# Queries and keys of seven head pairs as 2x2 block products ahead of the attention, in a two-branch encoder block

## The chip, the cores and the metric

One Trainium2 chip, one NeuronCore of it. The time is device microseconds of one execution; lower is better. PE is TensorE's matmul, PEld its weight load, DVE is VectorE, ACT ScalarE, POOL GpSimd, SP SyncE, which here issues most DMAs.

## The reference

One encoder layer on 1024 positions of 1024 channels, float32. Only the part up to the attention is touched by the change:

```python
h = rmsnorm(x, g_mix[i]) * (1 + scale1) + shift1
proj = h @ w_in[i]
qa, ka, va, qb, kb, vb, ga, gb = jnp.split(proj, split_at, axis=-1)
oa = mixture_of_dilations(heads(qa), heads(ka), heads(va), rel_bias)        # 8 heads of 64
ob = neighbourhood_attention_2d(heads(qb), heads(kb), heads(vb), na_rpb[i]) # 8 heads of 64
merged = jax.nn.sigmoid(ga) * (oa @ w_branch_dil) + jax.nn.sigmoid(gb) * (ob @ w_branch_na)
x = x + gate1 * (merged @ w_out[i])
...                                                                         # then a convolutional FFN
```

`w_in` has 40 column tiles of 128: 4 each of queries, keys and values of the dilated branch, 4 each of the neighbourhood branch, and 16 of gates. A tile of queries or keys holds one pair of heads.

## The kernel before

**Precision.** A float32 product is made of three matmuls of reduced-precision parts: `hi` is an operand rounded by ACT, `lo` what is left, by a subtraction on DVE or POOL; hi·hi, hi·lo and lo·hi are summed in PSUM (`product`, lines 84 to 86).

**Stages.** First (0 to 142 us) the modulated `h` is made, in two halves of 512 positions (`scaled`, `modulate`), then the values of all heads and the queries and keys of head pair 0. Then comes the attention, then the merge of the branches, `w_out`, and the FFN. The FFN's up and down projections already use block products in seven steps (`a_operands`, `products`, lines 1363 to 1365).

**Attention in slots.** It runs in 100 numbered slots. 64 belong to the dilated branch, eight per head; from slot 64 on the neighbourhood branch has four per head. In a slot PE makes scores `S` (from `qs`, `ks`, `kl`); DVE adds the bias and takes the minimum (L690, L1017); ACT takes exponentials (L691, L1019); two slots later PE turns the weights (`T`), ACT and DVE split them (`th` L698, `tl` L699), and in the slot after that PE multiplies by the values (`O`). A finished head output is taken by ACT and then DVE (`u`, L733 and L734; L1057 and L1061). In the neighbourhood branch DVE and POOL also normalise the weights (L1023, L1026).

**Filling.** Between these PE does other work in steps of three matmuls (`fill_steps`): 30 column tiles, 14 of queries and keys for the coming pairs and 16 of gates, each 16 steps (two halves, eight blocks of K). The loop at the end gives a slot 4, 8, 6 or 4 steps, spread over four places. For the neighbourhood queries `q_step` writes two half-wide matmuls in place of one, to reorder positions. Queries and keys are evicted by `q_evict` and `k_evict`, a half head at a time, into tiles for scores; keys are copied to the other partitions by DMA.

**Order.** PE, ACT and DVE run in the order in which the attention's code is written; SP and POOL are ordered by a scheduler. Work that isn't due at one moment (evictions, weight splits `whi`, value splits `vv`, outputs `u`, gate evictions `gs`) waits in a queue of pairs: `aside(ns, one, two)`. After each fill step `catch_up(550)` first emits all `two` parts of what was emitted before (DVE's half), then as many `one` parts (ACT's half) as 550 ns pay for. So the places of the fill steps set the places of these instructions.

**A pair's weights.** Per dilated pair, DVE writes row sums that go through DRAM and come back twice (`turn`, `factors`, `shares`, `weigh`), three and four slots later.

Of the kernel before, what the change touches and what calls it, by code (L numbers as in the profile page):

```python
# [29 lines left out]
def hybrid_encoder(tc, xT, c, w_ada, small, w_in, p1_bias, p23_bias, na_bias, ln2_mult, ident, w_br, w_out,  # L30
# [202 lines left out]
    def modulate(x, hf, ks, pb):  # L233

        last = ()
        for k in [*ks, None]:
# [7 lines left out]
            last = k is not None and (lo, t, b, f(hi))  # L244

    def scaled(x, k):

        hi, lo = h[0, k] = h_tile(), h_tile()
        t, b, g = stage[k % 2], ada[:, k:k + 1], am1[:, k:k + 1]
        act.activation(hi, x, AF.Identity, bias=b, scale=g)  # L250
# [106 lines left out]
    def at_once(ns, one, two=lambda: None):
        one()
        two()

    def q_evict(br, qk, hf, p, later=at_once):
        parts = []
        for i in range(2):
            a, b = slice(64 * i, 64 * i + 64), slice(64 - 64 * i, 128 - 64 * i)
            d, pp = qk[0][i][:, halves[hf]], p
            if br:
                d = qk[0][i].rearrange("p (v r t) -> p v r t", v=64, r=4)[:, :, 2 * hf:2 * hf + 2]
                pp = p.rearrange("p (r v t) -> p v r t", r=2, v=64)
            parts.append((d[a], d[b], pp[a]))

        def one():
            for da, db, pp in parts:
                act.activation(da, pp, AF.Copy)

        def two():
            for da, db, pp in parts:
                dve.tensor_tensor(db, pp, f(da), OP.subtract)
        later(1200, one, two)

    def k_evict(br, qk, hf, p, later=at_once):  # L380
        parts = []
        for i in range(2):
            a = slice(64 * i, 64 * i + 64)
            kh, ll, pp = qk[1][i][:, halves[hf]], qk[2][i][:, halves[hf]], p
            if br:
                kh, ll = (t.rearrange("p (w t r) -> p r w t", w=16, t=16)[:, 2 * hf:2 * hf + 2]
                          for t in (qk[1][i], qk[2][i]))
                pp = p.rearrange("p (r w t) -> p r w t", r=2, w=16)
            parts.append((kh[a], ll[a], pp[a]))

        def one(heads=(0, 1)):
            for kh, ll, pp in [parts[i] for i in heads]:
                act.activation(kh, pp, AF.Copy, scale=0.125)

        def two(heads=(0, 1)):
            for kh, ll, pp in [parts[i] for i in heads]:
                dve.scalar_tensor_tensor(ll, pp, 0.125, f(kh), OP.mult, OP.subtract)
            for i in heads:
                a, b = slice(64 * i, 64 * i + 64), slice(64 - 64 * i, 128 - 64 * i)
                for t in (qk[1][i], qk[2][i]):  # L400
                    if br == 0:
                        sp.dma_start(f(t)[b, halves[hf]], f(t)[a, halves[hf]])
                    elif hf:
                        sp.dma_start(f(t)[b], f(t)[a])
        if br == 0:
# [13 lines left out]

    def q_step(br, p, w, hf, k):  # L420
        if br == 0:
            product(p, w, lambda k: h[hf, k], ks=[k])
            return
        mhi, mlo = (t.rearrange("p (r w c t) -> p r c w t", r=2, w=16, c=4) for t in h[hf, k])
        for x, (ww, m) in enumerate(((w[0], mhi), (w[0], mlo), (w[1], mhi))):
            for r in range(2):
                pe.matmul(p[:, 256 * r:256 * r + 256], ww[:, k], m[:, r], start=k + x + r == 0,  # L427
                          stop=k == KT - 1 and x == 2, skip_group_check=True)
# [8 lines left out]
    def vb_chunks(cb):  # L437
        t0, n = NA_T0[cb], NA_NC[cb]
        for r in range(4):
            sp.dma_start(vb_s[cb].rearrange("(w t r) n -> r w t n", r=4, t=n)[r],  # L440
                         vb_c[256 * r:256 * r + 256].rearrange("(w t) n -> w t n", t=16)[:, t0:t0 + n])

    with tc.manual_schedule(engines={e.engine for e in (sp, act, dve, pool, pe)}):
# [53 lines left out]
        for q in range(4):  # L497
# [6 lines left out]
            low = [scaled(x[0][k], k) for k in ks]  # L504
            if q == 0:
# [104 lines left out]

        done_rows = 0
        folds = folds_in(early.tile([128, 512], FT, name="mt", bufs=3), 4)
        due = []
        for n, step in enumerate(v_steps[:10]):
            if step is None:
# [19 lines left out]
            done_rows = row_ends[n]  # L635
        act.activation(wpool.tile([128, KT], FT, name="rs", bufs=2), cs, AF.Exp)
# [4 lines left out]
        sm_pool = tc.alloc_tile_pool(name="sm", bufs=2, reuse_waits="tile")  # L641
        lnm = sm_pool.tile([128, 384], FT, name="lnm", bufs=1)
        sp.dma_start(lnm, ln2_mult)
        loads = [dil_loads(head) for head in range(2)]
# [15 lines left out]
    first_w = w_split(ahead.pop(1), pool)  # L660
# [4 lines left out]
    ps_n.release()  # L665

# [91 lines left out]
    class DilHead:  # L758
        def __init__(self, pair, pr, i, s0, u, st):
# [208 lines left out]
    class NaHead:  # L968
# [97 lines left out]
    def fill_steps():  # L1066
        jobs = []
        for n, gates in enumerate((2, 2, 2, 2, 2, 1, 1, 4)):
            if n < 7:
                br, pr = divmod(n + 1, 4)  # L1070
                jobs += [(x_ + pr, "qk"[y], n + 1) for y, x_ in enumerate(((0, 4), (12, 16))[br])]
            g0 = sum(1 for j in jobs if j[1] == "g")
            jobs += [(24 + g0 + t, "g", g0 + t) for t in range(gates)]
        w, raw = first_w, {1: ahead.pop(jobs[1][0])}
        w_mark = 0
        marks = [0, 0]
        for n, (t, kind, to) in enumerate(jobs):
            ensure(w_mark)
            if n + 1 < len(jobs):
                w_next = [wpool.tile([128, KT, 128], FR, name=x_) for x_ in ("whi", "wlo")]  # L1080
                w_mark = side_split(raw.pop(n + 1), *w_next)
            if n + 2 < len(jobs):
                raw[n + 2] = w_load(w_in[jobs[n + 2][0]])
            if kind == "q":
# [890 lines left out]
```

## Time and profile before

| | |
|---|---|
| runs (3), median | 1477.52 us (1476.70 to 1478.46) |
| span of the profiled execution | 1474.0 us (the page has no other time of it) |
| mean granted TensorE clock | 0.998 |
| moved by DMA | 210.75 MB, mean 143 GB/s |
| the chain that ended last | PE 90%, DVE 3%, DMA 3%, ACT 2% |
| S of the dilated branch | from 142.0 us |
| S of the neighbourhood branch | from 416.9 us |

The span runs from the first to the last instruction; the run times hold what lies around it too. Matmuls in a row overlap in the trace (a 512-wide one has 0.39 us and the next starts 0.23 us later), so the price of one is the distance of two starts. An idle time in brackets stands before the instruction, with the one that released it.

### The profile page before, as it was taken

How to read it: one execution, taken by the hardware profiler on the slowest of the kernel's cores; microseconds unless marked ns; L12 is line 12 of the kernel's file. 1: busy time of each engine (PE TensorE's matmuls, PEld its weight loads, DVE VectorE, ACT ScalarE, POOL GpSimd, SP SyncE). 2: the span in 40 equal slices, each digit the busy share in tenths (PEclk: the TensorE clock that was granted, in tenths of full speed). 3: DMA queues.
4: the chain of work that ended last, by engine and by line, in shares of the span. 5: the costliest groups of instructions: out<-in, count | busy, mean ns of one | idle time of the engine just before them, and what ended most of it. 6: DMA issues, size and time to landing. Idle time of an engine off the chain costs nothing.

```text
span 1474.0 us, 21562 instructions
## 1 busy us (share of the span) xinstructions
PE 1459.1 (99%) x7584; PEld 1242.1 (84%) x7584; DVE 943.2 (64%) x1775; ACT 775.8 (53%) x1448; POOL 766.6 (52%) x640
## 2 busy tenths in 40 slices
PE   9999999999999999999999999999999999999998
PEld 8888888889898998888888778888888888888888
DVE  7785546555654656466516897666666667787865
ACT  5522666666655666553346554444444447575543
POOL 4132333333234454422268678766676676989712
PEclk9999999999999999999999999999999999999999
DMA  9587325354736556587553313222222234542313
GB/s 371 199 305 260 91 84 129 99 136 126 194 110 176 142 147 172 164 260 256 192 165 127 107 53 133 86 86 86 86 73 81 72 130 142 200 128 87 107 41 115
DMA packets 121173, 210.75 MB, mean 143 GB/s; under 512 B 46660, under 2 KB 59588, under 8 KB 121028
## 3 DMA queue, kind: packets, MB, share of 16 engines
q1 hardware_dynamic: 119064, 206.41, 44.1%
q10 hardware_dynamic: 2000, 2.95, 0.5%
q8 instruction: 60, 0.98, 0.3%
q14 instruction: 49, 0.40, 0.1%
HBM read 163.58 MB, written 43.12 MB: 140 GB/s over the span
## 4 chain that ended last, share of the span: by engine, by line
PE 90%; DVE 3%; DMA 3%; ACT 2%; issue 1%; POOL 0%; SPq 0%; DVEq 0%; ACTq 0%; POOLq 0%
PE pj L1363 12%; PE pj L1364 12%; PE pj L1365 12%; PE pj L84 11%; PE pj L86 11%; PE pj L85 11%; PE pj L427 2%; PE O L1048 2%; PE T L1035 1%; PE S L1013 1%; PE pv L301 1%; PE pv L300 1%; PE pv L302 1%; PE O L876 1%; PE O L825 1%; PE T L859 1%
## 5 line engine op out<-in xcount | busy, mean ns | idle before, releaser
L61 POOL TENSOR_TENSOR wlo<-wraw,whi 128x512 fp32r<-128x512 f32 (+1 forms) x84 | 106.3, 1288 | 145.2 <-ACT whi L57 143.4
L84 PE MATMUL pj<-h,whi 128*128 128x512 f32 x432 | 178.0, 412 | 0.1
L86 PE MATMUL pj<-h,wlo 128*128 128x512 f32 x432 | 169.7, 393 | 0.0
L85 PE MATMUL pj<-h,whi 128*128 128x512 f32 x432 | 169.4, 392 | 0.0
L1364 PE MATMUL pj<-op,wsh 128*128 128x512 f32 x408 | 158.7, 389 | 0.5 <-DVE op L1290 0.5
L1363 PE MATMUL pj<-op,wsh 128*128 128x512 f32 x408 | 158.4, 389 | 0.5 <-ACT wsh L57 0.5
L1365 PE MATMUL pj<-op,wsl 128*128 128x512 f32 x408 | 157.4, 389 | 0.0
L699 DVE TENSOR_TENSOR tl<-T,th 128x512 fp32r<-128x512 f32 (+3 forms) x120 | 77.3, 654 | 106.9 <-ACT th L698 105.7
L749 POOL TENSOR_TENSOR wlo<-wraw,whi 128x512 fp32r<-128x512 f32 x58 | 74.2, 1294 | 131.7 <-ACT whi L748 131.7
L61 POOL TENSOR_TENSOR wsl<-big,wsh 128x512 fp32r<-128x512 f32 (+1 forms) x86 | 112.0, 1325 | 45.6 <-ACT wsh L57 40.7
L691 ACT ACTIVATE P<-P,st 128x256 f32<-128x256 f32 x128 | 64.2, 502 | 87.2 <-DVE st L690 87.2
L1599 DVE SCALAR_TENSOR_TENSOR big<-pj,sm,big 128x512 f32<-128x512 f32 (+2 forms) x183 | 94.9, 562 | 16.6 <-ACT big L1593 15.6
L86 PEld LDWEIGHTS pj<-h,wlo 128*128 128x128 f32 x432 | 81.1, 188 | 18.0
L84 PEld LDWEIGHTS pj<-h,whi 128*128 128x128 f32 x432 | 81.5, 189 | 11.3 <-issue 0.5
L1363 PE MATMUL pj<-op,whi 128*128 128x512 f32 x232 | 90.7, 391 | 0.2 <-ACT wc L1369 0.2
L1363 PEld LDWEIGHTS pj<-op,wsh 128*128 128x128 f32 x408 | 76.6, 188 | 16.9 <-ACT wsh L57 1.0
L1364 PEld LDWEIGHTS pj<-op,wsh 128*128 128x128 f32 x408 | 76.6, 188 | 16.7 <-DVE op L1290 0.9
L1365 PE MATMUL pj<-op,wlo 128*128 128x512 f32 x232 | 90.3, 389 | 0.0
L1364 PE MATMUL pj<-op,whi 128*128 128x512 f32 x232 | 90.3, 389 | 0.0
L85 PEld LDWEIGHTS pj<-h,whi 128*128 128x128 f32 x432 | 81.6, 189 | 10.1
L1365 PEld LDWEIGHTS pj<-op,wsl 128*128 128x128 f32 x408 | 76.6, 188 | 16.1 <-POOL wsl L61 0.2
L61 POOL TENSOR_TENSOR wsl<-wraw,wsh 128x384 fp32r<-128x384 f32 (+1 forms) x46 | 57.1, 1262 | 57.5 <-ACT wsh L57 49.9
(423 smaller groups left out, 4160.1 us busy)
## 6 DMA issues: line engine op xcount, KB each, us to landing
wraw<-w_in SPq DMA_DIRECT2D x32, 512.0 KB
wada<-w_ada SPq DMA_DIRECT2D x31, 512.0 KB
big<-w_up SPq DMA_DIRECT2D x22, 512.0 KB
wraw<-w_up SPq DMA_DIRECT2D x22, 512.0 KB
big<-as SPq DMA_DIRECT2D x22, 512.0 KB
as<-big SPq DMA_DIRECT2D x21, 512.0 KB
gs<-gs SPq DMA_DIRECT2D x32, 256.0 KB
g<-gs SPq DMA_DIRECT2D x16, 512.0 KB
```

What stands on the lines that cost most here:

```text
L61: lo_eng.tensor_tensor(lo[:, i:i + step], raw[:, i:i + step], f(hi)[:, i:i + step], OP.subtract)
L84: pe.matmul(psum, whi[:, k0 + k], mhi, start=k == 0, stop=False)
L85: pe.matmul(psum, whi[:, k0 + k], mlo, start=False, stop=False)
L86: pe.matmul(psum, wlo[:, k0 + k], mhi, start=False, stop=k == n - 1)
L427: pe.matmul(p[:, 256 * r:256 * r + 256], ww[:, k], m[:, r], start=k + x + r == 0, stop=k == KT - 1 and x == 2, skip_group_check=True)
L691: act.activation(pp, pp, AF.Exp, bias=mi, scale=-1.0, accum_out=li)
L699: dve.tensor_tensor(tl[:m, :n], pt[:m, :n], f(th)[:m, :n], OP.subtract)
L749: pool.tensor_tensor(lo[:, i:i + n], raw[:, i:i + n], f(hi)[:, i:i + n], OP.subtract)
L1363: pe.matmul(psum, whi[:, k], bhi, start=j < 4 and k == 0, stop=False, skip_group_check=True)
L1364: pe.matmul(psum, whi[:, k], blo, start=False, stop=False, skip_group_check=True)
L1365: pe.matmul(psum, wlo[:, k], bhi, start=False, stop=k == n - 1, skip_group_check=True)
L1599: dve.scalar_tensor_tensor(y[:, dst], src, wt, y[:, dst], OP.mult, OP.add)
```

## The change

Queries and keys of pairs 1 to 7 leave the filling. They are made in a stage of their own between the values and the attention, in the order 4, 5, 6, 7, 1, 2, 3. For a pair, the query tile and the key tile are the two block rows of the stationary operand, the halves of K its two block columns; the halves of positions are the block columns of `h`. Seven block products of 12 matmuls each replace eight (`STEPS`, moved up in the file). This needs:

- raw (unsplit) `h`, kept by extra ACT instructions (`keep_scaled`, and a line in `modulate`), four sums of blocks on POOL (`t_sums`, eight instructions of 1024 columns), and their splits (`t_split`: 16 times ACT, then DVE or POOL);
- per pair, three POOL sums, one DVE sum and seven halves of splits on ACT and POOL (`a_operands`), and five DVE additions and an ACT copy on PSUM (`products`);
- evictions of whole tiles, both heads at once (`qk_evict`, `na_evict`), stored in DRAM (`q_scr`), hi and lo, and loads by pair (`qk_load`), eight slots ahead of a pair's first slot.

In the attention 16 gate tiles are left: 256 steps. Five come ahead of slot 0, then 2, 4, 3 or 2 per slot, in fewer places: with two steps, one stands after the turns and one at the slot's end. `qk_marks` and the evictions in the slots are gone.

```diff
@@ modulate, scaled
+            if k is not None:
+                act.activation(raw_h[hf][k // 2][:, k % 2], t, AF.Identity, bias=b)
...
+    def keep_scaled(x, k):
+        act.activation(x, x, AF.Identity, bias=ada[:, k:k + 1], scale=am1[:, k:k + 1])
...
@@ evictions
+    def split_qk(y, dst, src):
+        hi, lo = dst
+        act.activation(hi, src, AF.Copy, scale=(1.0, 0.125)[y])
+        if y:
+            dve.scalar_tensor_tensor(lo, src, 0.125, f(hi), OP.mult, OP.subtract)
+        else:
+            dve.tensor_tensor(lo, src, f(hi), OP.subtract)
+
+    def qk_evict(pr, y, hf, p, tag):
+        st = qkpool.tile([128, 2, 512], FR, name=tag)
+        split_qk(y, (st[:, 0], st[:, 1]), p)
+        sp.dma_start(q_scr[pr, 2 * y:2 * y + 2].rearrange("x p s -> p x s")[:, :, halves[hf]], f(st))
...
+    def qk_load(pr):
+        qk = qk_tiles()
         for i in range(2):
             a = slice(64 * i, 64 * i + 64)
...
+            sp.dma_start(f(qk[0][i]), q_scr[pr, 0:2, a])
+            for y in range(2):
+                for b in range(2):
+                    sp.dma_start(f(qk[1 + y][i])[64 * b:64 * b + 64], q_scr[pr, 2 + y, a])
+        return qk
...
@@ sums of the blocks of h
+        def t_sums():
+            (a0, a1, c0, c1), (b0, b1, d0, d1) = raw_h
+            for a, b in ((a0, b0), (a1, b1)):
+                pool.tensor_tensor(a, b, a, OP.subtract)
+            for b, d in ((b0, d0), (b1, d1)):
+                pool.tensor_tensor(b, d, b, OP.subtract)
+            for a, d in ((a0, d0), (a1, d1)):
+                pool.tensor_tensor(d, d, a, OP.subtract)
+            for c, d in ((c0, d0), (c1, d1)):
+                pool.tensor_tensor(c, c, d, OP.subtract)
...
@@ the new stage, ahead of the attention
+    gens = [p_products(n, (0, 4, 1, 2, 3, 5, 6)) for n in range(2)]
+    for _ in range(2):
+        for g in gens:
+            advance(g)
+    t_split("T4", rpool, h0[2:], (dve, pool))
+    for n in range(len(order)):
+        if n + 2 < len(order):
+            raw[n + 2] = p_load(n + 2)
+        if n + 1 < len(order):
+            nxt = prep[1] if n == 0 else a_operands(raw.pop(n + 1), 4, p_home, p_sts[n + 1], spot=p_spot)
...
+        for j in gens[n] if n < 2 else p_products(n):
+            if j in (1, 2, 5):
+                next(nxt, None)
+            if n + 1 == len(order) and j == 2:
+                qk = qk_load(0)
...
@@ fill_steps
-        for n, (t, kind, to) in enumerate(jobs):
+        for n in range(16):
...
-                    q_step(int(kind == "q" and to > 3), p, w, hf, k)
+                    product(p, w, lambda k: h[hf, k], ks=[k])
...
@@ the loop over slots
+    for pr in range(1, 8):
+        at(16 * pr - 8 if pr < 5 else 8 * pr + 24, "first", qk_ahead, pr)
...
+    FIRST = 256 - 21 - 64 * 2 - 8 * 4 - 16 * 3 - 11 * 2
...
+    fill(FIRST)
     for s in range(100):
-        n = 4 if s < 64 else 8 if s < 72 else 6 if s < 88 else 4
+        n = 2 if s < 64 else 4 if s < 72 else 3 if s < 88 else 2
         run(slots[s]["first"])
         run(slots[s]["O"])
...
-        fill(n // 4, s not in late_slots)
+        fill(n > 2, s not in late_slots)
         for job in run(slots[s]["T"]):
             job()
...
-        fill(n // 4)
+        fill(1)
         run(slots[s]["late O"])
         run(slots[s]["S"])
         run(slots[s]["last"])
-        fill(n // 4)
+        fill(n > 3)
         for job in run(slots[s]["W"]):
             job()
-        fill(n - n // 4 * 3)
+        fill(1)
```

How this moves instructions, at slot 13 of the dilated branch. PE before, from the last score of the slot to the turn of the next:

```order
L843 MATMUL S_1998<-kl_726,qb_1068 128x256
L84 MATMUL pj_1934<-h_544,whi_1739 128x512
L85 MATMUL pj_1934<-h_545,whi_1739 128x512
L86 MATMUL pj_1934<-h_544,wlo_1740 128x512
L84 MATMUL pj_1934<-h_548,whi_1739 128x512
L85 MATMUL pj_1934<-h_549,whi_1739 128x512
L86 MATMUL pj_1934<-h_548,wlo_1740 128x512
L84 MATMUL pj_2018<-h_765,whi_1739 128x512
L85 MATMUL pj_2018<-h_766,whi_1739 128x512
L86 MATMUL pj_2018<-h_765,wlo_1740 128x512
L859 MATMUL T_2024<-idt_63,P_1959 128x128 x3
```

PE now, the same place (S_2985 and T_3006 are S_1998 and T_2024 there):

```order
L1028 MATMUL S_2985<-kl_2370,qb_2459 128x256
L84 MATMUL pj_2999<-h_315,whi_2688 128x512
L85 MATMUL pj_2999<-h_316,whi_2688 128x512
L86 MATMUL pj_2999<-h_315,wlo_2689 128x512
L1044 MATMUL T_3006<-idt_63,P_2949 128x128 x3
```

Of three steps between the score and the turn one is left; the step after the turn stays. DVE before, in the same slot, with a finished output (`u23`), the split of turned weights (`tl`) and the two minima with their results (`st`):

```order
L734 TENSOR_TENSOR u23_1421<-O_1901,u23_1421 64x512
L699 TENSOR_TENSOR tl_1987<-T_1981,th_1986 128x512
L690 ISA P_1999,st_1422<-S_1998,bias_1335 128x256
L690 ISA st_1422 128x1
L690 ISA P_1999,st_1422<-S_1998,bias_1335 128x256
L690 ISA st_1422 128x1
```

DVE now:

```order
L886 TENSOR_TENSOR tl_2970<-T_2964,th_2969 128x512
L921 TENSOR_TENSOR u23_2501<-O_2909,u23_2501 64x512
L877 ISA P_2986,st_2502<-S_2985,bias_2472 128x256
L877 ISA st_2502 128x1
L877 ISA P_2986,st_2502<-S_2985,bias_2472 128x256
L877 ISA st_2502 128x1
```

The output has moved from ahead of the split to between the split and the minima. ACT before, from that output's first half to the next slot's turn:

```order
L733 ACTIVATE u23_1421<-O_1901 64x512
L698 ACTIVATE th_1986<-T_1981 128x512
L691 ACTIVATE P_1999,st_1422<-P_1999,st_1422 128x256 x2
L1095 ACTIVATE gs_2014<-pj_1934 128x512
L656 ACTIVATE vv_1881<-vv_1881 128x8x64
L698 ACTIVATE th_2028<-T_2024 128x384
```

ACT now:

```order
L920 ACTIVATE u23_2501<-O_2909 64x512
L885 ACTIVATE th_2969<-T_2964 128x512
L1269 ACTIVATE gs_2977<-pj_2850 128x512
L878 ACTIVATE P_2986,st_2502<-P_2986,st_2502 128x256 x2
L935 ACTIVATE whi_2995<-wraw_2690 128x512
L885 ACTIVATE th_3010<-T_3006 128x384
```

The gate's eviction (`gs`) has moved from behind the exponentials to ahead of them; one split (`whi`) stands between the exponentials and the next turn.

More of the change, by code (lines that the diff above doesn't have):

```diff
@@ L352, in v_banks @@
         return [banks[st // 2][:, st % 2 * 256:st % 2 * 256 + 256] for st in range(4)]
+    q_scr = dram.tile([8, 4, 128, S], FT, name="qks")
     def qk_tiles():
         return [[qkpool.tile([128, S], FR, name=n) for _ in range(2)] for n in ("qs", "ks", "kl")] + [[]]
[L357 to L378, printed above, removed]
@@ L418, in q_blocks @@
         qk[3].append(q)
[L420 to L428, printed above, removed]
     def va_chunks(cc):
@@ new lines, in products, with bank, tmp @@
+    def products(st, n, moving, done, seq=range(7), in_psum=False, hold=None, spare=None, other=None):
+        p, c = {}, {}
+        def bank(x_):
+            p[x_] = ps.tile([128, 512], FT, name="pj", bufs=6)
+            return p[x_]
+        def tmp(x_):
+            c[x_] = hold[0] if hold and x_ == "t" else (x_ == "v" and other or wide)()
+            return c[x_]
+        for j in seq:
+            a, b = STEPS[j]
+            x_ = "abcdacd"[j]
+            psum = bank(x_) if j < 4 else p[x_]
+            whi, wlo = st[a]
+            for k in range(n):
+                bhi, blo = moving(b, k)
+                pe.matmul(psum, whi[:, k], bhi, start=j < 4 and k == 0, stop=False, skip_group_check=True)
+                pe.matmul(psum, whi[:, k], blo, start=False, stop=False, skip_group_check=True)
+                pe.matmul(psum, wlo[:, k], bhi, start=False, stop=k == n - 1, skip_group_check=True)
+                if k < n - 1:
+                    yield -1
+            if j == 0:
+                act.activation(tmp("t"), psum, AF.Copy)
+            elif j == 1:
+                dve.tensor_tensor(c["t"], psum, c["t"], OP.add)
+            elif j == 2:
+                dve.tensor_tensor(tmp("v"), psum, c["t"], OP.add)
+            elif j == 3:
+                dst = p["b"] if in_psum else spare() if spare else c["v"]
+                dve.tensor_tensor(dst, psum, c["v"], OP.add)
+                done(1, 1, dst)
+            elif j == 4 and hold:
+                act.activation(hold[1], psum, AF.Copy)
+                done(0, 0, hold[1])
+            elif j == 4:
+                done(0, 0, psum)
+            elif j == 5:
+                dve.tensor_tensor(psum, psum, c["t"], OP.add)
+                done(0, 1, psum)
+            else:
+                dst = psum if in_psum or spare else c["t"]
+                dve.tensor_tensor(dst, psum, c["t"], OP.add)
+                done(1, 0, dst)
+            yield j
@@ L640, in hybrid_encoder, with t_split @@
         early.release()
[L641 to L644, printed above, removed]
+        lpool = tc.alloc_tile_pool(name="tops", bufs=1, reuse_waits="tile")
+        tops = {}
+        def t_split(n, tp, src, eng):
+            tops[n] = []
+            for k in range(4):
+                t = tp.tile([128, 2, 512], FR, name="op", bufs=8)
+                act.activation(t[:, 0], src[k // 2][:, k % 2], AF.Copy)
+                eng[k % 2].tensor_tensor(t[:, 1], src[k // 2][:, k % 2], f(t)[:, 0], OP.subtract)
+                tops[n].append((t[:, 0], t[:, 1]))
     def vb_load(head, vr):
@@ L658, in v_tile @@
         return vv
-    first_w = w_split(ahead.pop(1), pool)
+    (h0, h1) = raw_h
+    raw[1] = p_load(1)
+    t_split("T2", lpool, h1[2:], (dve, dve))
+    t_split("T1", lpool, h0[:2], (dve, dve))
+    prep = [a_operands(raw.pop(0), 4, p_home, p_sts[0], spot=p_spot)]
+    for _ in range(4):
+        next(prep[0])
     for br, st in v_steps[10:]:
```

297 lines of the change are left out of this document (140 added, 157 removed).

## The prediction, written before the change was run

> **What bounds the kernel now.** I read the busy shares first, then the stretches of the span, then who waited for whom, and last the instructions in order of time. All rows of this part are of the kernel before.
>
> ```profile
> PE 1459.1 (99%) x7584; PEld 1242.1 (84%) x7584; DVE 943.2 (64%) x1775; ACT 775.8 (53%) x1448; POOL 766.6 (52%) x640
> ...
> 142.00:417.00 275.00, 273.44 (x1654) 238.99 (x1653) 147.42 (x430) 177.56 (x455) 96.08 (x86) 1.00 0.45 123
> 417.00:612.00 195.00, 194.94 (x1234) 175.39 (x1233) 113.30 (x297) 120.18 (x282) 89.22 (x79) 1.00 0.56 157
> 900.00:1000.00 100.00, 100.00 (x443) 82.81 (x442) 64.02 (x101) 44.91 (x56) 75.32 (x59) 1.00 0.27 92
> ```
>
> The first row is the whole span; the others give, for a stretch, busy PE, PEld, DVE, ACT, POOL, the granted clock, the DMA share and GB/s. TensorE never stands still, so work taken from it looks like time saved. But the two attention stretches are full only because projection matmuls are poured into them. What lies under that filling shows in the waits (total, times, longest) between 140 and 640 us:
>
> ```profile
> DVE tl L699 <- ACT th L698: 105.7, 69, 4.2
> ACT P L691 <- DVE st L690: 87.2, 64, 1.9
> DVE P L690 <- PE S L802: 12.9, 15, 6.0
> DVE P L690 <- PE S L843: 7.0, 16, 0.6
> ```
>
> Dilated attention has 64 slots. In each of them ACT's exponentials wait for DVE's bias-and-minimum, and in nearly each DVE's `tl` waits for ACT's `th`; only in 31 does DVE wait for a score from PE. ACT and DVE take turns: a chain. Both engines run in order, so a slot can't be shorter than one round of it. In these rows the round is read off (start, duration):
>
> ```profile
> 376.37 0.60 ACT L698 ACTIVATE th<-T 128x512 fp32r<-128x512 f32 x1
> 378.68 0.51 ACT L691 ACTIVATE P<-P,st 128x256 f32<-128x256 f32 x1 [1.09 <-DVE st L690]
> 379.80 1.07 ACT L393 ACTIVATE ks<-pj 64x512 fp32r<-64x512 f32 x1
> 384.88 1.14 ACT L748 ACTIVATE whi<-wraw 128x512 fp32r<-128x512 f32 x2
> 386.05 0.60 ACT L698 ACTIVATE th<-T 128x512 fp32r<-128x512 f32 x1
> 388.86 0.59 ACT L733 ACTIVATE u<-O 64x512 f32<-64x512 f32 x1
> 389.48 0.28 ACT L698 ACTIVATE th<-T 128x128 fp32r<-128x128 f32 x1
> 389.65 0.59 ACT L1095 ACTIVATE gs<-pj 128x512 f32<-128x512 f32 x1
> ...
> 377.00 0.69 DVE L699 TENSOR_TENSOR tl<-T,th 128x512 fp32r<-128x512 f32 x1 [1.34 <-ACT th L698]
> 377.63 0.68 DVE L734 TENSOR_TENSOR u<-O,u 64x512 f32<-64x512 f32 x1
> 378.24 0.41 DVE L690 CUSTOM_DVE_ANT_0 P<-S,bias 128x256 f32<-128x256 f32 x1
> ...
> 387.42 0.66 PE L813 MATMUL T<-idt,P 128*128 128x128 f32 x4 [1.02 <-DVE tl L699]
> ```
>
> Start to start: `th` to `tl` 0.63, `tl` to the next DVE instruction 0.63 or 0.61, the minimum to the first exponential 0.44, both exponentials up to the next reader of PSUM 1.12. A bare round is 0.63 + 0.61 + 0.44 + 1.12 = 2.80 us. A head's output `u` adds 0.62 on ACT (388.86 to 389.48) and 0.63 on DVE (377.63) if it stands inside the round. The last row shows the chain over PE already: where key evictions made rounds too long at 387 us, PE stood for 1.02 us.
>
> **The change, part by part.**
>
> Matmul price first: the last step before a transpose, and the extents of the stages.
>
> ```profile
> 200.22 0.39 PE L84 MATMUL pj<-h,whi 128*128 128x512 f32 x1
> 202.30 0.60 PE L859 MATMUL T<-idt,P 128*128 128x128 f32 x4
> ...
> L801 PE MATMUL S<-ks,qs x64: 274/282/335, 142.0 to 394.7; 128*128 128x256 f32 x64
> L1013 PE MATMUL S<-ks,qs x64: 291/320/394, 416.9 to 612.2; 128*128 128x288 f32 x32, 128*128 128x384 f32 x32
> ...
> 419.78 0.39 PE L427 MATMUL pj<-h,whi 128*128 128x256 f32 x2
> 420.01 0.40 PE L427 MATMUL pj<-h,wlo 128*128 128x256 f32 x2
> ```
>
> Nine fill matmuls take 2.08 us, 0.231 each, a fill step of three 0.693; two half-wide ones of the neighbourhood queries cost as much as one (0.23). In the dense stretch from 900 to 1000 us a 512-wide matmul takes 100/443 = 0.226.
>
> *Removed:* 14 tiles x 2 halves x 24 = 672 matmuls, 155.2 us, from the attention. *Added ahead of it:* 7 pairs x 7 steps x 12 = 588, at 0.226 132.9 us. TensorE alone would gain 22 us.
>
> The Trainium skill, page "TensorE: Matmul & The Clock Gate", section "Wait — 56ns, not 53.3ns?", has 215.7 ns from start to start for 512 columns; its price for the 588 would be an estimated 126.8 us, a sum 6 us lower. The rows show 10 ns more per matmul and stand.
>
> *Dilated slots.* 142.0 to 416.9 us are 64 slots of 4.30 us: four steps (2.77) and 1.52 of the slot's own matmuls. With two steps PE needs 2.91. The chain now: the order shows that with the middle fills gone each `u` on ACT stands between the exponentials and `th`, and its DVE half between `tl` and the minimum. A head of eight slots is 8 x 2.80 = 22.4, four `u` at 1.25 = 5.0, one weight split and one value split still inside at about 0.46 (1.17/2 from 384.88 to 386.05, less the 0.12 by which a PSUM reader starts later) = 0.9, and 0.17 for the ninth, narrow turn: 28.5 us, 3.56 a slot; 3.6 with the pair's small copies. The gates' evictions and the other splits stand behind `th`, where ACT waits 1.09 us anyway. Since 3.6 > 2.91, PE waits about 0.7 us in each slot. Lower bound 2.91 (PE), upper bound 4.30 (as now); I take 3.6, the sum of rows. 64 x 3.6 less 3 us for two first slots without a turn = 227.4, against 274.9: **-47.5 us**, where PE alone would give -88.7.
>
> *Neighbourhood slots.* 195.3 us for 31 slots; fill 188 steps = 130.3, so 2.10 of its own per slot. PE needs 4.87, 4.18 and 3.49 us with 4, 3 and 2 steps. The chain here:
>
> ```profile
> 573.85 0.62 ACT L1019 ACTIVATE P<-P,stb 128x384 f32<-128x384 f32 x1 [2.00 <-DVE stb L1017]
> 575.06 0.58 ACT L1095 ACTIVATE gs<-pj 128x512 f32<-128x512 f32 x1
> 576.06 0.58 ACT L698 ACTIVATE th<-T 96x512 fp32r<-96x512 f32 x1
> 577.76 0.54 ACT L1019 ACTIVATE P<-P,stb 128x288 f32<-128x288 f32 x1 [0.61 <-DVE stb L1017]
> ...
> 571.39 1.29 DVE L699 TENSOR_TENSOR tl<-T,th 96x512 fp32r<-96x512 f32 x2 [2.29 <-ACT th L698]
> 572.60 0.74 DVE L1061 TENSOR_TENSOR u<-O,u 64x256 f32<-64x256 f32 x2
> 577.28 0.44 DVE L1017 CUSTOM_DVE_ANT_0 P<-S,bias 128x288 f32<-128x288 f32 x1
> ```
>
> Exponentials 1.21, `th` to the minimum 1.22, the minimum to the exponential 0.48: 2.9; every second slot has a second turn (+0.61) and, with three steps or more, an output inside (0.74 on DVE, about 0.65 on ACT); a gate or split costs 0.5 (575.06 to 576.06 holds two). Laid over the order this gives 4.2 per slot with three steps, 3.9 with two. So 8 x 4.95 + 16 x 4.4 (both limits close together) + 7 x 3.9 = 137.3: **-58.0 us** (by PE alone 130.3). The last four slots go from 4.87 to 3.9, and one more step is left for behind: **-3.2**.
>
> *Product stage.* 132.9 us if PE is fed. A pair needs ten POOL instructions:
>
> ```profile
> L61 POOL TENSOR_TENSOR wlo<-wraw,whi 128x512 fp32r<-128x512 f32 (+1 forms) x84 | 106.3, 1288 | 145.2 <-ACT whi L57 143.4
> ...
> 840.00:860.00 20.00, 17.96 (x79) 14.21 (x78) 19.97 (x28) 12.01 (x19) 7.35 (x5) 1.00 0.09 27
> ```
>
> 10 x 1.29 = 12.9 us against 19.0 of matmuls; ACT's and DVE's parts are smaller. Stationary tiles are reused one pair later, and the new split (about 1 us on ACT, 2.6 on POOL) has three products, 8.1 us, to hide in. The same scheme in the up projection lost 2.04 us in its worst start (second row). I add 3 (0 to 15): **+135.9**.
>
> *Opening of the attention.* Five steps, 3.5 us, stand ahead of the first score to cover loads of bias and values: **+3.5** (0 to 8).
>
> *Copies for the block sums.* Eight ACT copies per half.
>
> ```profile
> 34.59 0.82 ACT L250 ACTIVATE h<-ks,ada,am 128x512 fp32r<-128x512 f32 x1 [2.34 <-DVE ada L317]
> 65.02 0.69 ACT L241 ACTIVATE h<-pv,ada 128x512 fp32r<-128x512 f32 x1 [0.75 <-DVE pv L240]
> ...
> 120.91 2.54 POOL L61 TENSOR_TENSOR wlo<-wraw,whi 128x512 fp32r<-128x512 f32 x2 [17.28 <-ACT whi L57]
> ```
>
> In the first half two copies (1.4 us) meet an idle 2.34, in the second one copy of 0.69 meets 0.75 per block. The eight double-width sums, 8 x 2.58 = 20.6 us of POOL, mostly fall into the 17.28 us in which it idles; the first pair's ten instructions (12.9 us) then have the 21 us from 121 to the stage's start at 142. **+1** (0 to 4) for the place before the second value weights where ACT has no gap.
>
> *Transfers.* Per pair 1 MB of weights and 2 MB of stores go into the product stage, and in the slots 3 MB of loads replace 1 MB of copies and two weight tiles of 0.5 MB: 1 MB more in 16 slots of 3.6 us, 17 GB/s on top of 123 (which the shorter slots raise to some 147). SP issues them between its own:
>
> ```profile
> 212.99 0.49 SPq L908 DMA_DIRECT2D sts<-fs  x1
> 216.31 2.87 SPq L914 DMA_DIRECT2D fs<-sts  x8
> ```
>
> The weights' round trip is issued by 219.2 us, 6.2 us after its start; DVE reads it three slots on, 10.8 us. I cost it at nothing; if loads ahead of it make it late, DVE, then ACT's `th`, then PE wait (0 to 12 us in all).
>
> **Sum:** -47.5 - 58.0 - 3.2 + 135.9 + 3.5 + 1.0 = +31.7 us. On the profiled span of 1474.0 that is 1505.7; the median of the runs, 1477.5, has 3.5 more around it: **1509 us**.
>
> **The rivals.**
>
> *PE stays the bound (faster).* If outputs and evictions hide beside the chain, slots cost 2.91 and 4.87/4.18/3.49: 186.2 + 130.3 + 14.0 for what was 489.7, so -88.7 - 65.0 - 4.8 + 140.4 = -18, 1459 us. It decides below 3.1 us per dilated slot, where the sum is zero. For it: PE is full now. Against it: the chain is measured, and PE's 1.02 us.
>
> *A shorter chain, about 3.2 us a slot:* 64 x 0.4 = 26 less, 1483.
>
> *Products wait for operands.* If POOL or the reused tiles cost 2.5 us a pair, +17: 1526. The 2.04 us above speak for it, the 12.9 against 19.0 not.
>
> *Late transfers* at the pairs' factors and the biases: +12, 1521.
>
> *The clock.* The stretch 142 to 417, with the wait of 1.02 us in it, has granted clock 1.00. Were the clock halved by PE's new waits, a dilated slot's 2.91 became 5.8: 64 x 2.2 = +141, 1650 us. The Trainium skill (same page, "What's actually happening") states that a TensorE idle for a window of about 3.4 us falls to half its clock; by that rule, waits of 0.7 us don't do it, and the trace so far agrees.
>
> **How the numbers follow.** Forecast 66% (1495 to 1525), shorter chain 10, PE-bound 6, operands 9, transfers 7, clock 2. The range 1484 to 1530 takes in the forecast, half of the shorter chain, and most of operands and transfers, 80%. About 0.2% (3 us) can be told from no change. Faster: PE-bound and a fifth of the shorter chain, 8%; same 4%; slower 88%.
>
> **What would show it.** Right: first dilated to first neighbourhood score some 227 us apart; PE about 80% busy there, its waits released by DVE `tl`; the product stage near 136 us with PE full; clock 1.00. Wrong: slots near 2.9 us with PE full, or gaps inside the product stage, or waits released by DMA.

## The result, and the profile after

The changed kernel takes 1658.87 us (median of four runs, 1656.75 to 1660.42) against 1477.7: ratio 1.1231, 95% interval 1.1215 to 1.1247. The forecast was 1509 us, 1484 to 1530. The sign was right; the loss is 181 us instead of 32. The profiled execution has a span of 1654.9 us, against 1474.0.

First the extents of the stages in the kernel after: the first product, the last group of products, the dilated scores (L987) and the neighbourhood's scores (L1197), each with count, duration and first and last start.

```profile
152.09 0.39 PE L499 MATMUL pj<-h,whi 128*128 128x512 f32 x1
...
L501 PE MATMUL pj<-op,kl x112: 388/389/398, 159.3 to 293.3; 128*128 128x512 f32 x112
L987 PE MATMUL S<-ks,qs x64: 278/283/550, 309.9 to 577.4; 128*128 128x256 f32 x64
L1197 PE MATMUL S<-ks,qs x64: 291/338/689, 592.7 to 793.0; 128*128 128x288 f32 x32, 128*128 128x384 f32 x32
```

The first score stands 167.9 us later than before (forecast 140.4); the dilated stretch takes 282.8 us, longer than the 274.9 it took with twice the filling (forecast 227.4); the neighbourhood 200.3 against 195.3 (forecast 137.3); what lies behind is unchanged. So the price ahead of the attention was paid and nothing came back. The page says what took it: the share of PE, the chain that ended last by engine, and by line.

```profile
PE 1496.4 (90%) x7308; PEld 1250.3 (76%) x7308; DVE 985.8 (60%) x1805; ACT 782.6 (47%) x1463; POOL 851.8 (51%) x694
...
PE 58%; DMA 22%; DVE 6%; ACT 5%; POOL 4%; issue 2%; SPq 2%; DVEq 0%; ACTq 0%; POOLq 0%
PE pj L499 12%; PE pj L501 12%; PE pj L500 12%; DMA qs<-qks 5%; PE pj L84 5%; PE pj L86 5%; PE pj L85 5%; DMA bias<-na_bias 4%; DMA qks<-qs 2%; DMA gs<-gs 2%; DMA wraw<-w_in 1%; DMA fb<-fcs 1%; DMA sts<-fs 1%; PE O L1232 1%; DVE tl L886 1%
```

22% of the chain are DMAs, and first among them is `qs<-qks`, the load of the prepared queries. The waits between 290 and 810 us (total, times, longest) name its victims, the biases of both branches:

```profile
DVE tl L886 <- ACT th L885: 140.5, 91, 12.5
...
POOL bias L974 <- DMA bias<-p_bias: 70.0, 5, 28.6
...
DVE P L1201 <- DMA bias<-na_bias: 60.5, 8, 13.8
```

The longest wait of `tl` for `th` is 12.5 us where it was 4.2: ACT stood in front of it. How that comes about is seen in order of time, on SP's queue, ACT, PE and POOL:

```profile
329.28 0.53 SPq L1270 DMA_DIRECT2D gs<-gs  x1
...
334.64 13.18 SPq L402 DMA_DIRECT2D qs<-qks  x2
347.91 10.19 SPq L1270 DMA_DIRECT2D gs<-gs  x1
...
375.09 0.33 SPq L695 DMA_DIRECT2D bias<-p_bias  x1
...
375.81 0.60 ACT L1269 ACTIVATE gs<-pj 128x512 f32<-128x512 f32 x1 [12.20 <-DMA gs<-gs]
...
381.77 1.00 POOL L974 TENSOR_TENSOR bias<-bias,lnm 128x384 f32<-128x384 f32 x1 [28.65 <-DMA bias<-p_bias]
```

SP needs 13.18 us to issue two query loads, then 10.19 for a store of gates, where the one before took 0.53. Everything behind it in the queue moves back: the bias's second half goes out at 375.09, and POOL, which adds a mask to it, has then waited 28.65 us. ACT waits 12.20 us to evict a gate, because the store that frees its tile is stuck too; and since ACT works in order, exponentials and `th` stand behind that eviction. What the DMA engines do meanwhile stands in two stretches (busy PE, PEld, DVE, ACT, POOL, clock, DMA share, GB/s):

```profile
350.00:356.00 6.00, 5.93 (x38) 5.26 (x39) 2.96 (x12) 3.85 (x12) 3.12 (x3) 1.00 0.13 52
...
366.00:374.00 8.00, 0.29 (x2) 0.00 (x0) 0.00 (x0) 0.00 (x0) 0.00 (x0) 0.68 0.33 97
```

A DMA share of 0.13 is two engines of 16. Transfers are late here while most of the DMA engines are idle, so bandwidth is not what is lacking; it suggests that a transfer is carried by few of them, which the next runs test. The query load is the one access of the change whose outermost dimension is 2 (`q_scr[pr, 0:2, a]`, 2 x 64 x 1024); the key loads beside it have 64 rows outermost. The Trainium skill, page "DMA: Bandwidth & Descriptors", section "Why a DMA increments its semaphore by 16 and not by 1", states that a DMA runs on the largest number of engines up to 16 that divides the outermost sizes of both sides. By that rule it is 2 here; the share of 0.13 agrees.

### The profile page after: what moved, and what is told of

It reads as the page before. It is cut to its first block, busy times and chain, and to the rows that moved or that the text cites. A ratio compares the mean times of both kernels' runs of the same rounds, so it can differ in the third digit from the quotient of the medians.

```text
span 1654.9 us, 21287 instructions
## 1 busy us (share of the span) xinstructions
PE 1496.4 (90%) x7308; PEld 1250.3 (76%) x7308; DVE 985.8 (60%) x1805; ACT 782.6 (47%) x1463; POOL 851.8 (51%) x694
## 4 chain that ended last, share of the span: by engine, by line
PE 58%; DMA 22%; DVE 6%; ACT 5%; POOL 4%; issue 2%; SPq 2%; DVEq 0%; ACTq 0%; POOLq 0%
PE pj L499 12%; PE pj L501 12%; PE pj L500 12%; DMA qs<-qks 5%; PE pj L84 5%; PE pj L86 5%; PE pj L85 5%; DMA bias<-na_bias 4%; DMA qks<-qs 2%; DMA gs<-gs 2%; DMA wraw<-w_in 1%; DMA fb<-fcs 1%; DMA sts<-fs 1%; PE O L1232 1%; DVE tl L886 1%
## 5 line engine op out<-in xcount | busy, mean ns | idle before, releaser
L61 POOL TENSOR_TENSOR wlo<-wraw,whi 128x512 fp32r<-128x512 f32 (+1 forms) x92 | 116.7, 1290 | 142.2 <-ACT whi L57 140.4
L61 POOL TENSOR_TENSOR wsl<-big,wsh 128x512 fp32r<-128x512 f32 (+1 forms) x86 | 111.2, 1315 | 44.4 <-ACT wsh L57 39.4
L84 PE MATMUL pj<-h,whi 128*128 128x512 f32 x272 | 123.5, 454 | 0.0
L86 PE MATMUL pj<-h,wlo 128*128 128x512 f32 x272 | 113.2, 416 | 0.0
L85 PE MATMUL pj<-h,whi 128*128 128x512 f32 x272 | 113.0, 415 | 0.0
L1210 POOL TENSOR_SCALAR P<-P,stb 128x288 f32<-128x288 f32 (+1 forms) x32 | 40.5, 1265 | 107.2 <-DVE stb L1207 61.4
L500 PEld LDWEIGHTS pj<-op,wsh 128*128 128x128 f32 x408 | 76.6, 188 | 16.8 <-DVE op L1468 0.9
L61 POOL TENSOR_TENSOR wsl<-wraw,wsh 128x384 fp32r<-128x384 f32 (+1 forms) x46 | 56.8, 1255 | 57.1 <-ACT wsh L57 52.8
L1203 ACT ACTIVATE P<-P,stb 128x288 f32<-128x288 f32 (+1 forms) x64 | 36.4, 569 | 99.2 <-DVE stb L1201 99.2
L57 ACT ACTIVATE whi<-wraw 128x1024 fp32r<-128x1024 f32 (+2 forms) x49 | 48.5, 994 | 67.9 <-PE pj L85 30.4
L1672 ACT ACTIVATE big<-pj,sm 128x512 f32<-128x512 f32 x61 | 47.0, 772 | 53.3 <-DVE pj L520 32.0
```

What stands on the lines that cost most here:

```text
L57: act.activation(hi, raw, AF.Copy)
L61: lo_eng.tensor_tensor(lo[:, i:i + step], raw[:, i:i + step], f(hi)[:, i:i + step], OP.subtract)
L84: pe.matmul(psum, whi[:, k0 + k], mhi, start=k == 0, stop=False)
L85: pe.matmul(psum, whi[:, k0 + k], mlo, start=False, stop=False)
L86: pe.matmul(psum, wlo[:, k0 + k], mhi, start=False, stop=k == n - 1)
L500: pe.matmul(psum, whi[:, k], blo, start=False, stop=False, skip_group_check=True)
```

## The experiments

**Splitting the query loads** (`load_split`).

```diff
-            sp.dma_start(f(qk[0][i]), q_scr[pr, 0:2, a])
+            for x_ in range(2):
+                sp.dma_start(f(qk[0][i])[64 * x_:64 * x_ + 64], q_scr[pr, x_, a])
```

> Only the query loads of a head pair change: each 128x1024 tile comes as two loads of 64 rows instead of one load whose source is 2 x 64 x 1024. Theory (the load with an outer dimension of 2 is carried by two of the core's 16 DMA engines, some 50 GB/s, 10 us for 512 KB, and what is queued behind it on these two lands late): a load lands in 3 to 4 us, the waits for bias, fb, gs and ks in the attention nearly go, first dilated to first neighbourhood score about 235 us instead of 283, neighbourhood about 145 instead of 200, the whole 1515 to 1560 us. Rival (the added megabytes and SP's longer list are the cost, however they are spread): within 10 us of 1659. Rival (the chain of ACT and DVE is longer than I laid it out): DMA waits go, but the dilated stretch stays over 265 us and the time over 1600.

1542.96 us; ratio to before 1.045, interval 1.0433 to 1.0467. Two lines give back 116 of the 181 us. Extents of its products and its scores, and its dilated stretch:

```profile
150.81 0.39 PE L500 MATMUL pj<-h,whi 128*128 128x512 f32 x1
...
L502 PE MATMUL pj<-op,kl x112: 388/389/397, 158.0 to 291.9; 128*128 128x512 f32 x112
L988 PE MATMUL S<-ks,qs x64: 278/282/416, 296.2 to 505.8; 128*128 128x256 f32 x64
L1198 PE MATMUL S<-ks,qs x64: 291/339/628, 522.9 to 677.4; 128*128 128x288 f32 x32, 128*128 128x384 f32 x32
296.00:523.00 227.00, 205.30 (x1209) 165.44 (x1207) 123.12 (x397) 147.32 (x406) 78.66 (x72) 0.98 0.71 181
```

The dilated stretch is now 226.7 us (forecast 227.4), the neighbourhood 154.5. More DMAs, the same bytes, a DMA share of 0.71 instead of 0.57 in the dilated slots: not the bytes but their spread cost these 116 us. The waits for biases shrank less than expected: `p_bias` fell from 70.0 to 24.6 us, `na_bias` from 60.5 to 25.4, and the neighbourhood stayed above the 145 of the theory. Of the 113.1 us between the two spans, 56.1 lie in the dilated stretch, 45.8 in the neighbourhood and 13.7 ahead of the first score (behind, 2.5 were lost).

**The form of the transfer by itself** (`before_two`, `before_four`, `before_sixteen`): the kernel before, with 14 needless copies of 512 KB from DRAM to DRAM that differ in shape alone.

```diff
+    d_scr = dram.tile([8, 4, 128, S], FT, name="dum")
+
+    def extra(pr):
+        for i in range(2):
+            sp.dma_start(d_scr[pr, 0:2, 64 * i:64 * i + 64], w_in[pr].rearrange("(b p) k m -> b p (k m)", b=2))
+    for pr in range(1, 8):
+        at(16 * pr - 8 if pr < 5 else 8 * pr + 24, "first", extra, pr)
```

This is `before_two`. `before_four` writes `d_scr[pr, 0:4, 32 * i:32 * i + 32]` with `b=4`, and `before_sixteen` writes `d_scr[pr, i]`, 128 rows of 1024; source and target have the same shape each time.

> The kernel before, with 14 needless copies of 512 KB from DRAM to DRAM, two per head pair where the changed kernel loads queries, each shaped 2 x 64 x 1024 at its target. Theory of the two engines: each copy holds two engines for 10 us or more with a DMA share near 0.13, and biases, value rows and the weights' round trip queued behind it come late: 10 to 100 us slower. Rival of the volume: the same as the run with 128 rows, within 3 us.

> The same 14 copies of 512 KB in the kernel before, shaped 128 x 1024. Theory of the two engines: spread over all, a copy takes 3 to 4 us and hides: within 3 us of before. Rival of the volume: as slow as the run with 2 x 64 x 1024, 10 us or more.

> The kernel before with the same 14 copies of 512 KB, shaped 4 x 32 x 1024 at the target. With 2 rows outside they cost 131.7 us, with 128 rows 18.8, all in one piece near the start. If the outer dimension sets how many DMA engines carry a copy, 4 of 16 give half the 131.7, so some 60 to 70 us: 1537 to 1550 us. If the cost of the 2 x 64 x 1024 form comes from something else in the form (a slow issue of three dimensions), it stays near 1608.

1608.73 us (ratio 1.0896, interval 1.088 to 1.0912), 1542.58 (1.0449, 1.0428 to 1.047) and 1495.86 (1.0133, 1.0117 to 1.0148): +131.7, +65.3 and +18.8 us on 1477.05, 1477.28 and 1477.05, in the order two, four, 128 rows. The copies depend on nothing, so SP's scheduler issued them all near the start, ahead of loads that PE needs, and not in the slots where I had meant them; nothing hides them there, and the runs became a price list. SP issues ten copies in a row from about 39 us; then copies and needed loads alternate. SP's queue in `before_two` and a stretch in which only copies are issued, then the same of `before_four`:

```profile
82.29 0.60 SPq L1117 DMA_DIRECT2D dum<-w_in  x1
91.98 0.32 SPq L145 DMA_DIRECT2D wada<-w_ada  x1
101.58 0.60 SPq L1117 DMA_DIRECT2D dum<-w_in  x1
...
120.00:140.00 20.00, 0.00 (x0) 0.00 (x0) 0.00 (x0) 0.00 (x0) 0.00 (x0) 0.50 0.12 54
```

```profile
63.44 0.61 SPq L1117 DMA_DIRECT2D dum<-w_in  x1
68.31 0.32 SPq L145 DMA_DIRECT2D wada<-w_ada  x1
73.09 0.63 SPq L1117 DMA_DIRECT2D dum<-w_in  x1
...
84.00:92.00 8.00, 0.00 (x0) 0.00 (x0) 0.00 (x0) 0.00 (x0) 0.00 (x0) 0.50 0.22 95
```

Behind the ten copies SP issues one DMA, copy or load, every 9.65 us with 2 outside and every 4.83 with 4. I read the step as the time of one copy ahead in the queue: 14 of them are 135 and 68 us, near the 131.7 and 65.3 that the runs lost. 512 KB in 9.65 us are 54 GB/s, as the 54 of the row and the 52 of the kernel after. With 4 outside the DMA share is 0.22 instead of 0.12 and the time half: the outer size sets how many engines carry the copy. With 128 the runs lost 18.8/14 = 1.34 us per copy; that is a cost, not a duration that was seen. `before_two` lost more than the 10 to 100 us expected, and the expectation that 14 copies over all engines would hide within 3 us was wrong, since none had cover where they ran. (`before_four` was run twice, the others four times.)

**The block sums** (`sums_dve`): the eight sums of the modulated input by DVE instead of POOL (`pool.tensor_tensor` to `dve.tensor_tensor` in `t_sums`), on top of the split loads.

> The kernel with split query loads, and the eight block sums of the modulated input on DVE instead of POOL. In that kernel DVE's weight splits beside POOL's sums took 2.84 us instead of 0.68 to 0.9 and four row sums 11.1 us instead of 3.1, and the products begin at 150.8 us where the kernel before starts its attention at 142.0. Theory (POOL and DVE on SBUF tiles slow each other): the sums cost DVE about 11 us, of which it has 12 idle between 100 and 140 us; the products begin 5 to 9 us earlier, 1534 to 1539 us against 1543. Rival (the sums' work is late wherever it runs, or the weights' transfers set the start): within 2 us of 1543.

1537.3 us, ratio 1.041 (1.0392 to 1.0427): 5.7 us less. The products begin at 146.7 instead of 150.8. DVE in `load_split`, then POOL beside it; then in `sums_dve` the first products and DVE:

```profile
96.74 2.83 DVE L61 TENSOR_TENSOR vwl<-kl,vwh 128x512 fp32r<-128x512 f32 x1
...
105.05 0.68 DVE L373 TENSOR_TENSOR kl<-pj,kl 128x512 fp32r<-128x512 f32 x1
...
107.58 11.13 DVE L674 SCALAR_TENSOR_TENSOR sq<-wada,cs,sq 128x512 f32<-128x512 f32 x4
...
96.23 5.58 POOL L702 TENSOR_TENSOR ks<-qs,ks 128x1024 f32<-128x1024 f32 x2
```

```profile
L500 PE MATMUL pj<-h,whi x56: 389/389/499, 146.7 to 280.9; 128*128 128x512 f32 x56
...
96.87 0.68 DVE L61 TENSOR_TENSOR vwl<-kl,vwh 128x512 fp32r<-128x512 f32 x1
```

Beside POOL's sums a DVE instruction took 2.83 us instead of 0.68, and four row sums 11.13; each lasts as long as one of POOL's (2.79). POOL's work was not free cover: it slowed DVE, for whose weight splits PE waits 3.7 us between 80 and 152 us in `load_split` and 0.5 in `sums_dve`. The products begin 4.1 us earlier, a little less than the 5 to 9 expected.

**The burst or the bytes** (`spread_loads`): a pair's six tiles of 512 KB loaded one per slot.

```diff
...
-        at(16 * pr - 8 if pr < 5 else 8 * pr + 24, "first", qk_ahead, pr)
+        for n in range(6):
+            at((16 * pr - 8 if pr < 5 else 8 * pr + 24) + n, "first", qk_piece, pr, n // 3, n % 3)
```

> The kernel with split query loads, and the six 512 KB tiles of a pair loaded one per slot over six slots instead of 3 MB at once. Theory (in the neighbourhood the burst fills the DMA engines, share 0.87 to 1.08 between 572 and 620 us, and the biases behind it land late: 25 us of waits for na_bias): these waits fall below 8 us, the neighbourhood's scores go from 154.5 to about 142, 1528 to 1535 us. Rival (the sum of bytes, not the burst, fills the engines): waits and time stay within 3 us of 1543.

1542.85 us, ratio 1.0447 (1.0426 to 1.0467): nothing. The waits for `na_bias`, between 290 and 700 us:

```profile
DVE P L1202 <- DMA bias<-na_bias: 18.1, 7, 7.1
...
POOL P L1211 <- DMA bias<-na_bias: 11.5, 1, 11.5
```

29.6 us, no less than the 25.4 of the split loads (rows below); the neighbourhood takes 156.7 us. The rival held. Together with the sums on DVE (`dve_and_spread`):

> Split query loads, block sums on DVE, and loads spread over six slots, together. If both theories hold the gains add up: 1520 to 1530 us, still slower than before, since the dilated chain (226 us for what needs 186 of PE) is untouched. Rivals: one of the two gains or none appears, 1535 to 1545.

1536.68 us (1.0402, 1.0384 to 1.0419), which is `sums_dve` alone: one of the two gains, as the rival had it.

**Fewer bytes** (`keys_once`): keys loaded for the first pair alone.

```diff
+        qk[1:3] = k_first
...
-            for y in range(2):
+            for y in range(2 if pr == 0 else 0):
```

> The kernel with split query loads, in which the key tiles are loaded for the first pair alone and used for all eight (the other pairs' keys are left out): 1 MB of loads per pair instead of 3, everything else the same. Theory (in the neighbourhood the bytes fill the DMA engines, and biases land late): the waits for na_bias fall from 25 us to under 5, the neighbourhood's scores go from 154.5 to 138 to 145, the time to 1525 to 1533 us. Rival (the neighbourhood is that long by its chain, as I should have laid it out): within 4 us of 1543, whatever the waits say.

1525.92 us, ratio 1.0329 (1.0308 to 1.0349): 17 us less than the split loads. The waits of `load_split` between 515 and 700 us and its DMAs from 578 to 618, then, of `keys_once`, the waits between 290 and 700 us, the neighbourhood's scores and their stretch:

```profile
DVE P L1202 <- DMA bias<-na_bias: 16.4, 6, 4.9
...
POOL P L1211 <- DMA bias<-na_bias: 9.0, 1, 9.0
...
DMA packets 6985, 9.88 MB, mean 247 GB/s; under 512 B 4154, under 2 KB 4154, under 8 KB 6982
...
q1 hardware_dynamic: 6982, 9.84, 98.6%
```

```profile
POOL P L1216 <- DMA bias<-na_bias: 4.3, 1, 4.3
...
DVE P L1207 <- DMA bias<-na_bias: 1.0, 1, 1.0
L1203 PE MATMUL S<-ks,qs x64: 291/338/389, 526.1 to 664.6; 128*128 128x288 f32 x32, 128*128 128x384 f32 x32
526.00:665.00 139.00, 135.58 (x828) 118.75 (x828) 92.83 (x280) 94.03 (x250) 74.30 (x66) 1.00 0.70 194
```

In the neighbourhood a pair comes every eight slots, and with 3 MB per pair the DMA engines are full from 578 to 618 us (98.6%) at 247 GB/s, with 4154 of 6985 packets under 512 bytes. Without the keys the waits fall from 25.4 to 5.3 us and the scores go from 154.5 to 138.5 us, near the forecast's 137.3. That doesn't show the forecast's chain there: PE is busy for 135.58 of these 139.00 us.

**What sets a dilated slot** (`one_step`, `half_u`). One gate step per dilated slot with the other 64 run ahead; and DVE's half of each dilated output left out:

```diff
-    FIRST = 256 - 21 - 64 * 2 - 8 * 4 - 16 * 3 - 11 * 2
+    FIRST = 256 - 21 - 64 * 1 - 8 * 4 - 16 * 3 - 11 * 2
...
-        n = 2 if s < 64 else 4 if s < 72 else 3 if s < 88 else 2
+        n = 1 if s < 64 else 4 if s < 72 else 3 if s < 88 else 2
...
-        fill(1)
+        if n > 1:
+            fill(1)
+        else:
+            catch_up(550)
```

```diff
-                             lambda: dve.tensor_tensor(dst, po[0:64], dst, OP.add)))
+                             lambda: None))
```

> The kernel with split query loads, and one gate step instead of two in each of the 64 dilated slots; the 64 steps taken out (44.4 us at 0.693) run ahead of the first slot. Theory (the chain of ACT and DVE sets a dilated slot at 3.5 us, PE's own need is 2.91): the dilated stretch stays at 215 to 226 us, so nearly all of the 44 us is added: 1575 to 1587 us. Rival (PE's filling still sets the slot): the stretch shrinks by about 44 us and the time stays at 1543.

> The kernel with split query loads, in which the dilated outputs keep ACT's half alone; DVE's half of each output (0.62 us, four per head of eight slots) is left out. Theory (the round of ACT and DVE sets the dilated slot, and an output stands in it): 64 x 0.31 = 20 us less at most, bounded below by the 3.28 us per slot that one gate step left; dilated stretch 207 to 217 instead of 226.5, time 1523 to 1534 us. Rival (PE or late loads set the slot): within 3 us of 1543.

`one_step` takes 1573.64 us (1.0654, 1.0637 to 1.0671), 31 us more than the split loads. Its first dilated and first neighbourhood scores:

```profile
L988 PE MATMUL S<-ks,qs x64: 277/283/428, 348.4 to 540.3; 128*128 128x256 f32 x64
L1198 PE MATMUL S<-ks,qs x64: 291/339/629, 558.3 to 714.9; 128*128 128x288 f32 x32, 128*128 128x384 f32 x32
```

The stretch is 209.9 us, so 16.8 of the 44.4 us moved ahead came back. `half_u` takes 1524.48 (1.032, 1.0296 to 1.0344):

```profile
L988 PE MATMUL S<-ks,qs x64: 278/282/415, 300.4 to 493.3; 128*128 128x256 f32 x64
L1198 PE MATMUL S<-ks,qs x64: 290/339/629, 507.9 to 664.1; 128*128 128x288 f32 x32, 128*128 128x384 f32 x32
```

207.5 us, 19.2 less; the step's price was 64 x 0.31 = 20. Work of DVE that isn't on PE at all shortens the stretch by nearly its full length, while 44 us taken from PE shorten it by 17. And the 17 aren't PE's alone, since the steps took work of ACT with them. The gates' evictions in the dilated stretch, in `load_split` and in `one_step`:

```profile
L1270 ACT ACTIVATE gs<-pj 128x512 f32<-128x512 f32 x16 | 9.4, 586 | 0.0
...
L1270 ACT ACTIVATE gs<-pj 128x512 f32<-128x512 f32 x8 | 4.7, 591 | 0.0
```

The weight splits `whi` fall from 11.0 to 4.9 us, so ACT has 10.8 us less to do; and a wait of PE for ACT of 4.05 us in the first slots of `load_split` (its row stands further down) is not in the stretch of `one_step`. So the chain of ACT and DVE sets the dilated slot. Whether PE's second step adds anything beside it, these runs don't tell: with both steps and half the output `half_u` needs 3.24 us a slot, `one_step` 3.28. `one_step` came out a little below its theory (215 to 226, 1575 to 1587), which had not counted ACT's part.

None of these beats the kernel before, and the measured pieces say why: the products cost 141 us, and what the attention returned in these runs, with every product ahead of it, was 48.2 us in the dilated slots and, even without the keys' bytes, 56.8 in the neighbourhood: 105.

## Why the prediction was wrong, step by step

Times in us. "After" and "split" are the changed kernel and the one with split query loads, both against the kernel before.

| term | forecast | after | split | what the runs showed |
|---|---|---|---|---|
| copies, start of the products | +1.0 | +10.1 | +8.8 | 4.1 of it go with the sums on DVE |
| product stage | +135.9 | +141.4 | +141.3 | full from 200 to 280 us, gaps before |
| opening | +3.5 | +16.4 | +4.1 | query and key loads late |
| dilated slots | -47.5 | +7.9 | -48.2 | chain right; hidden by late transfers |
| neighbourhood slots | -58.0 | +5.0 | -40.8 | -56.8 without the keys' bytes |
| behind | -3.2 | +0.1 | +2.6 | not followed up |
| sum | +31.7 | +180.9 | +67.8 | |

*Transfers: the step that failed.* "I cost it at nothing", with "0 to 12 us in all", was worked out from a mean, 17 GB/s on top of 123. The time of a transfer is not in that number. The load `q_scr[pr, 0:2, a]` ran on two engines, 9.65 us for 512 KB by the copies' price, sixteen times; the spans of after and split lie 113 us apart. The rival "late transfers" named the right victims, factors and biases, and gave them 12 us and 7 in 100. What should have been looked at is each new transfer's outermost size, which the diff shows.

*The same step, a second time.* "1 MB more in 16 slots" is true of the dilated branch. In the neighbourhood a pair lasts eight slots, so the rate is twice that, on engines that were already busy 0.56 of the time. Without key loads the neighbourhood takes 138.5 instead of 154.5 us. These 16.0 us are the price of all key loads, 2 of the 3 MB; what the overlooked part alone cost was not measured.

*Copies: +1 forecast, 8.8 measured.* The sums "mostly fall into the 17.28 us in which it idles" took POOL's idle time for free time; DVE paid. The Trainium skill, page "SBUF — State Buffer", section "Who interferes with whom", states that a DVE instruction with two SBUF inputs contends with a POOL instruction that reads SBUF; the 2.83 against 0.68 us agree. The other 4.7 us of the term are not explained by a run.

*Product stage:* 135.9 forecast, 141.3 measured; 10 x 1.29 against 19.0 held once the stage ran, and the gaps lie at its beginning, as two stretches of split show:

```profile
180.00:200.00 20.00, 17.38 (x67) 13.24 (x67) 8.01 (x11) 6.66 (x9) 12.07 (x10) 0.91 0.49 157
...
200.00:280.00 80.00, 80.00 (x355) 66.25 (x354) 35.01 (x51) 30.57 (x44) 50.05 (x41) 1.00 0.54 183
```

PE's waits in the stage are 0.74, 1.28, 0.41 and 2.12 us, for splits of POOL and ACT and for an addition of DVE: 4.6 of the 8.4 us by which it exceeds the 132.9 of its matmuls. Behind the last of them the clock is halved for 3.4 us (rows below), an estimated 1.7 us more (half of 3.4). So "products wait for operands" was true in a small way, and the 3 us allowed for it were too few.

*Chain:* 227.4 forecast, 226.7 in split; 137.3 forecast, 138.5 without the keys' bytes. `half_u` shows that the chain sets the dilated slots. That the sum met the measurement within 1 us is partly luck: the 226.7 hold the wait of 4.05 us in the first slots, which the forecast didn't have, and without it a slot takes 3.48 us, not 3.55. In the neighbourhood PE's own price was put at 130.3 us, too near the chain's to tell them apart where PE is busy for 135.58.

*The rivals.* "PE stays the bound" is out for the dilated slots by `one_step`, where 44.4 us less of PE gave 16.8, and by `half_u`; "a shorter chain" of 3.2 us a slot by the 226.7 us, 3.54 a slot. "Products wait for operands" had 17 us on a term that rose by 5.4. "The clock" had 1650 us, near the measured time, by another way: it halved the clock through short waits. That is refuted in split. Two of PE's longer waits, the clock behind the first of them, and the dilated slots without the start:

```profile
192.12 0.50 PE L500 MATMUL pj<-op,kl 128*128 128x512 f32 x1 [2.12 <-ACT kl L57]
...
303.43 1.39 PE L1000 MATMUL T<-idt,P 128*128 128x128 f32 x4 [4.05 <-ACT P L879]
...
193.00:196.40 3.40, 3.30 (x9) 2.53 (x9) 0.84 (x2) 1.09 (x1) 1.66 (x2) 0.50 0.98 233
308.00:523.00 215.00, 197.37 (x1177) 159.23 (x1175) 118.29 (x381) 140.54 (x389) 71.69 (x66) 1.00 0.70 177
```

From 308 to 523 us, with waits of up to 1.35 us, the clock is 1.00; the stretch's mean of 0.98 comes from the wait of 4.05 us ahead of that. In after the clock falls in the long gaps (0.68 at 366 to 374 us, where PE ran 0.29 of 8 us). The Trainium skill, page "TensorE: Matmul & The Clock Gate", section "What's actually happening", has the halved clock after an idle window of some 3.4 us; here a wait of 2.12 us was enough for it. The fall is a consequence of the late transfers: the same 7308 matmuls keep PE busy for 1496.4 instead of 1478.0 us, 18 us that the slower clock may have added to the waits.

*What would show it:* waits "released by DMA" were listed as the sign of being wrong, and they were it. Of the signs of being right, the 227 us came with split; PE was to be about 80% busy there and was so for 205.30 of 227.00 us, 90%. Its waits were released by DVE `tl`, as forecast, for 15.8 of 21.1 us.

Open: 4.7 us at the start of the products, some 2 in their stage and 5.8 behind the attention.

## What to carry to other kernels

Price each new transfer by its own shape before its bytes: outermost size first, since it sets how many DMA engines carry it, then its rate in the stretch where it runs, not in the mean. Where waits for DMA stand beside a DMA share near 2/16, look for the access with a 2 outside, and split it. A queue that is in order passes one slow transfer on to all that stand behind it, so the victim in the list of waits (here a bias, a store of gates) need not be the cause.

## What the hardware showed that I had not expected

A 512 KB copy cost 9.65, 4.83 and 1.34 us with 2, 4 and 128 rows outside. The fast ones ran so (`before_sixteen`, 36 to 58 us):

```profile
36.00:58.00 22.00, 22.00 (x164) 20.63 (x163) 12.96 (x19) 11.52 (x19) 5.53 (x4) 1.00 1.03 376
```

With the slow loads SP itself stood for 13.18 us in issuing two of them, so that transfers behind them were not even started while the DMA share was 0.13.

DVE instructions on two SBUF tiles took 2.83 us beside POOL's sums and 0.68 without; one that read PSUM and one SBUF tile, while POOL's sums ran, kept its 0.68 (`kl<-pj` at 105.05).

The neighbourhood's DMA engines were full at 247 GB/s, where the copies over 128 rows reached 376 (share 1.03): with 4154 of 6985 packets under 512 bytes, here the share and not GB/s told that they were full.
